# Twelve rows of the first block loaded through GpSimd's queue in transfers of 5, 120 and 3 partitions

## Chip, cores and metric

One core of one Trainium2 chip. The metric is the device time of one execution in microseconds (us), median of several executions. Times inside a run are us from the start of the profiled span, which is 1.2 to 1.7 us shorter than the device time.

## The reference

```python
W_adapted = W + scale * (lora_A @ lora_B)            # 256 x 256, rank 16
W_norm = np.sqrt(np.sum(W_adapted ** 2, axis=0, keepdims=True) + 1e-8)
W_final = W_adapted / W_norm * m
y = x.reshape(-1, 256) @ W_final                     # x: 16 x 2048 x 256 float32
```

The weights are small. The work is to read 33.5 MB of x, multiply it by a 256 x 256 matrix, and write 33.5 MB of y.

## The kernel before

x is cut into 8 blocks of 128 partitions x 32 rows x 1 KB (4 MB; the last is loaded and stored in two halves). There are five block buffers, and the result overwrites the block's buffer. SyncE (queue q1 in the profile) issues the loads, ACT (q10) the stores. GpSimd casts to bfloat16, TensorE transposes and multiplies, DVE and ACT move the results back.

```python
def load_x(n):
    nc.sync.dma_start(
        out=in_sbuf(*parts[n]), in_=in_dram(x_flat, *parts[n])
    ).then_inc(sem(f"load{n}"), 16)
...
for n in range(len(parts)):
    b = parts[n][0] // CH
    if b >= XBUFS and parts[n][0] % CH == 0:
        nc.sync.wait_ge(sem(f"store{b - XBUFS}"), 16)   # buffer free again
    load_x(n)
...
for p in range(NPR):                                    # GpSimd, four casts a block
    b, c = divmod(p, PRB)
    if p == 0 or part_of[2 * p - 1] != part_of[2 * p]:
        nc.gpsimd.wait_ge(sem(f"load{part_of[2 * p]}"), 16)
    if p >= NXB:
        nc.gpsimd.wait_ge(sem("turned"), p - NXB + 1)
    nc.gpsimd.tensor_copy(out=xb_bufs[p % NXB][:],
        in_=x_bufs[b % XBUFS][:, 2 * c * J : 2 * (c + 1) * J, :],
    ).then_inc(sem("rounded"), 1)
```

So loads 0 to 4 are issued at once, load 5 only when store 0 has landed, load 6 after store 1, and loads 7 and 8 after store 2.

## Time and profile before

| | before |
|---|---|
| device time, median of 3 runs | 164.33 us (163.7 to 165.0) |
| span of the profiled run | 163.2 us |
| mean DMA rate over the span | 413 GB/s |
| first cast / first store issued / last store issued | 13.83 / 34.52 / 148.20 us |

A line of the order of time gives start, duration, engine, line of the program, operation, and in brackets the engine's idle time before it with what ended it.

The stage of the early loads, in the table of stages whose columns the prediction explains:

```profile
12.00:32.00 20.00, 12.35 (x86) 10.38 (x87) 10.80 (x9) 5.60 (x6) 11.39 (x6) 1.00 0.99 426
```

Here only loads run, at 426 GB/s.

### The profile page before, as it was taken

Reading aid. Unit: us, or ns where it says so; the run is one execution under the profiler, and the core shown is the slowest. Engines: PE = TensorE matmul, PEld = TensorE weight load, DVE = VectorE, ACT = ScalarE, POOL = GpSimd, SP = SyncE. Lnnn points to the kernel's source line nnn. Section 1 sums busy time; section 2 is a strip of 40 time slices with the busy share of each in tenths; the row PEclk is TensorE's granted clock in tenths of the full one; section 3 lists DMA queues with packets and bytes.
Section 4 is the critical chain, followed back from the end, with each engine's and each line's share of the span. In section 5 each row is a group of like instructions: output and inputs, shape, how many; then the busy total and the mean of one; then the engine's idle time right before and its main releaser. Section 6 shows DMA issues by size and latency. Waiting matters only on the chain. (4 is left out here: it accounts for less than half of the span.)

```text
span 163.2 us, 1988 instructions
## 1 busy us (share of the span) xinstructions
PE 105.3 (65%) x786; PEld 85.2 (52%) x786; DVE 47.2 (29%) x44; ACT 63.8 (39%) x67; POOL 62.5 (38%) x39
## 2 busy tenths in 40 slices
PE   1270599789789897898981998619988820892000
PEld 0130577677577775776760867418676610771000
DVE  0429452350532514405230325005051400330000
ACT  3010027548366384473754053900738440062000
POOL 1006381753935738268004940069209003900000
PEclk9999999999999999999998589985899996599755
DMA  5998998998999999999999999999999999998991
GB/s 201 402 498 386 426 474 385 482 418 265 466 426 426 442 410 466 426 394 482 418 426 442 420 426 458 402 458 410 446 414 454 414 446 422 450 442 377 442 430 60
DMA packets 2915, 67.41 MB, mean 413 GB/s; under 512 B 465, under 2 KB 482, under 8 KB 610
## 3 DMA queue, kind: packets, MB, share of 16 engines
q1 hardware_dynamic: 1440, 33.82, 49.0%
q10 hardware_dynamic: 1474, 33.59, 47.8%
q14 instruction: 1, 0.01, 0.0%
HBM read 33.85 MB, written 33.55 MB: 413 GB/s over the span
## 5 line engine op out<-in xcount | busy, mean ns | idle before, releaser
L219 ACT COPY x_sb<-y_ps 128x1024 f32<-128x1024 f32 x64 | 61.9, 1014 | 75.8 <-PE y_ps L281 75.8
L165 POOL CAST xb<-x_sb 128x2048 bf16<-128x2048 f32 x32 | 60.0, 1902 | 79.3 <-DMA x_sb<-in_x_dram 56.0
L281 PE MATMUL y_ps<-w_final,xt 128*128 128x256 bf16 x512 | 64.6, 280 | 12.8 <-PEq L256 12.8
L202 DVE COPY xt<-xt_ps 128x1024 f32<-128x1024 f32 x32 | 38.2, 1221 | 88.1 <-PE xt_ps L267 88.0
L281 PEld LDWEIGHTS y_ps<-w_final,xt 128*128 128x128 bf16 x512 | 48.4, 100 | 28.2 <-issue 19.8
L267 PE MATMUL xt_ps<-identity,xb 128*128 128x128 f32 x264 | 39.1, 309 | 23.1 <-PEq L256 23.1
L267 PEld LDWEIGHTS xt_ps<-identity,xb 128*128 128x128 f32 x264 | 34.9, 161 | 25.8 <-issue 25.6
L198 DVE TENSOR_TENSOR w_final<-wam,rnorm 128x256 bf16<-128x256 f32 x2 | 4.0, 2028 | 0.0
L244 PE MATMUL y_ps<-sq,ones 128*128 128x256 f32 x4 | 2.1, 674 | 1.6 <-DVE sq L187 1.6
L233 PE MATMUL y_ps<-identity,a_nat 128*16 128x128 f32 x2 | 0.6, 397 | 3.6 <-DMA a_nat<-in_lora_A_dram 3.6
L212 ACT ACTIVATE norm<-y_ps,eps_col 128x256 f32<-128x256 f32 x1 | 0.5, 473 | 6.1 <-PE y_ps L244 6.1
L244 PEld LDWEIGHTS y_ps<-sq,ones 128*128 128x128 f32 x4 | 1.2, 323 | 2.3 <-DVE sq L187 2.1
L210 ACT ACT_TABLE_LOAD x1 | 1.3, 1283 | 2.4 <-issue 2.4
L233 PEld LDWEIGHTS y_ps<-identity,a_nat 128*16 128x16 f32 x2 | 0.1, 90 | 3.6 <-issue 3.6
L171 POOL MEMSET xb<- 128x2048 bf16 x1 | 1.8, 1805 | 0.3 <-PE xt_ps L267 0.3
L195 DVE RECIPROCAL rnorm<-norm 128x256 f32<-128x256 f32 x1 | 1.7, 1745 | 0.0
L237 PE MATMUL y_ps<-b_bf,aT 16*128 16x256 bf16 x2 | 0.6, 404 | 1.5 <-DVE aT L180 1.5
L189 DVE COPY m_all<-y_ps 128x256 f32<-128x256 f32 x1 | 0.4, 425 | 3.3 <-PE y_ps L249 3.3
L178 DVE CAST b_bf<-b_nat 16x256 bf16<-16x256 f32 x1 | 0.3, 281 | 3.8 <-DMA b_nat<-in_lora_B_dram 3.8
L249 PE MATMUL y_ps<-m_row,ones 1*128 1x256 f32 x2 | 1.2, 710 | 0.0
L237 PEld LDWEIGHTS y_ps<-b_bf,aT 16*128 16x128 bf16 x2 | 0.1, 106 | 1.9 <-DVE aT L180 1.9
L183 DVE SCALAR_TENSOR_TENSOR wa<-y_ps,w_nat 128x512 f32<-128x512 f32 x1 | 0.7, 692 | 0.8 <-PE y_ps L237 0.8
(13 smaller groups left out, 3.7 us busy)
## 6 DMA issues: line engine op xcount, KB each, us to landing
x_sb<-in_x_dram SPq DMA_DIRECT2D x7, 4096.0 KB, 27.1
out_dram<-x_sb ACTq DMA_DIRECT2D x7, 4096.0 KB, 37.2
x_sb<-in_x_dram SPq DMA_DIRECT2D x2, 2048.0 KB, 29.6
out_dram<-x_sb ACTq DMA_DIRECT2D x2, 2048.0 KB, 20.2
w_nat<-in_W_dram SPq DMA_DIRECT2D x1, 256.0 KB, 2.9
a_nat<-in_lora_A_dram ACTq DMA_DIRECT2D x1, 16.0 KB, 2.6
b_nat<-in_lora_B_dram ACTq DMA_DIRECT2D x1, 16.0 KB, 3.6
m_row<-in_m_dram ACTq DMA_DIRECT2D x1, 1.0 KB
```

The costliest lines, as they stand in the source:

```text
L165: nc.gpsimd.tensor_copy(out=xb_bufs[p % NXB][:], in_=x_bufs[b % XBUFS][:, 2 * c * J : 2 * (c + 1) * J, :],).then_inc(sem("rounded"), 1)
L171: nc.gpsimd.memset(xb_bufs[NPR % NXB][:], 0.0).then_inc(sem("rounded"), 1)
L183: nc.vector.scalar_tensor_tensor(out=wa[:], in0=ab_ps, scalar=float(scale), in1=w_nat[:], op0=ALU.mult, op1=ALU.add).then_inc(dv, 1)
L195: nc.vector.reciprocal(out=rnorm[:], in_=norm[:]).then_inc(dv, 1)
L198: i = nc.vector.tensor_mul(out=w_final[:, t], in0=wam[:, t], in1=rnorm[:])
L202: nc.vector.tensor_copy(out=xt_bufs[p % NXT][:].rearrange("p r t -> p (r t)").bitcast(FP32), in_=xt_ps[p % 2][:],).then_inc(sem("copied"), 1)
L210: nc.scalar.activation(out=warm[:], in_=eps_col[:], func=AF.Sqrt)
L219: nc.scalar.copy(out=x_bufs[b % XBUFS][:, c * J : (c + 1) * J, :], in_=y_ps[g % 2][:]).then_inc(sem("room"), 1)
L244: i = nc.tensor.matmul(n2_ps, ones[:], sq[:, t, :], start=(t == 0), stop=(t == KC - 1))
L249: nc.tensor.matmul(mb_ps, ones[0:1, :], m_row[:], start=True, stop=True).then_inc(pe, 1)
L267: i = nc.tensor.transpose(xt_ps[p % 2][:, j * P : (j + 1) * P], xb_bufs[p % NXB][:, j, :].bitcast(FP32), identity[:],)
L281: i = nc.tensor.matmul(y_ps[h][:, j, :], xt_bufs[p % NXT][:, r : r + P, t], w_final[:, t, :], start=(t == 0 and (j % (J // 2)) == 0), stop ...
```

## The change

One of the 16 DMA engines finishes the kernel later than the others. The intent is to give it less: 12 of 32 rows of block 0 are taken from the ordinary load, which is shared evenly, and loaded by GpSimd in three transfers arranged so that DMA engine 4 gets almost none of them.

```diff
+    EARLY = 12
+    SPARE = 4
+    SHARES = [(0, SPARE + 1), (SPARE + 1, 120), (SPARE + 121, 7 - SPARE)]
@@ load_x
+        s = EARLY if n == 0 else 0
         nc.sync.dma_start(
-            out=in_sbuf(*parts[n]), in_=in_dram(x_flat, *parts[n])
+            out=in_sbuf(*parts[n])[:, s:, :], in_=in_dram(x_flat, *parts[n])[:, s:, :]
         ).then_inc(sem(f"load{n}"), 16)
@@ GpSimd, after the identity and ahead of the casts
+    for k, (p0, cnt) in enumerate(SHARES):
+        nc.gpsimd.dma_start(
+            out=in_sbuf(*parts[0])[p0 : p0 + cnt, 0:EARLY, :],
+            in_=in_dram(x_flat, *parts[0])[p0 : p0 + cnt, 0:EARLY, :],
+            max_dma_last_dim=4096,
+        ).then_inc(sem(f"early{k}"), 16)
+    for k in range(len(SHARES)):
+        nc.gpsimd.wait_ge(sem(f"early{k}"), 16)
```

The cap of 4096 cuts each partition's 12 KB into three pieces.

## The prediction

> **What bounds the kernel now.** I read the page's slices first, then the table of stages, then the packets of two short windows, then the order of time on GpSimd and ACT.
>
> The slices (busy tenths of the mean DMA engine, and GB/s, in 40 equal parts of the span):
>
> ```profile
> DMA  5998998998999999999999999999999999998991
> GB/s 201 402 498 386 426 474 385 482 418 265 466 426 426 442 410 466 426 394 482 418 426 442 420 426 458 402 458 410 446 414 454 414 446 422 450 442 377 442 430 60
> ...
> q1 hardware_dynamic: 1440, 33.82, 49.0%
> q10 hardware_dynamic: 1474, 33.59, 47.8%
> ```
>
> See that the DMA engines are full from the second slice to the last but one, while no compute engine is over 65%: loads (q1) and stores (q10) take 96.8% of sixteen engines' span. So the time is bytes per DMA engine plus a start and a tail. Stages (us; busy time of PE, PEld, DVE, ACT, POOL with counts; granted clock; DMA share; GB/s):
>
> ```profile
> 114.00:135.00 21.00, 15.65 (x125) 12.23 (x123) 5.35 (x5) 11.76 (x12) 4.98 (x3) 0.96 1.02 439
> ...
> 148.50:159.40 10.90, 0.00 (x0) 0.00 (x0) 0.00 (x0) 0.00 (x0) 0.00 (x0) 0.71 0.99 424
> 159.40:160.50 1.10, 0.00 (x0) 0.00 (x0) 0.00 (x0) 0.00 (x0) 0.00 (x0) 0.50 0.25 104
> 160.60:162.70 2.10, 0.00 (x0) 0.00 (x0) 0.00 (x0) 0.00 (x0) 0.00 (x0) 0.50 0.05 23
> ```
>
> All compute is over by 148.5; then stores drain at full rate to 159.4, and from 160.6 to 162.7 the share is 0.05, about 1/16. One DMA engine works alone. Its packets:
>
> ```profile
> DMA packets 4, 0.05 MB, mean 23 GB/s; under 512 B 1, under 2 KB 1, under 8 KB 1
> ...
> q10 hardware_dynamic: 4, 0.05, 5.5%
> ```
>
> Three packets of 16 KB and one semaphore write. In the packet records (start and duration, without engine numbers) sixteen last-store semaphore writes end at 159.57 to 160.42 us, but the last at 162.78: a straggler 2.36 us behind the next. Following its packets back by end-meets-start, it never idles. It does its equal share more slowly: 32 KB packets that last 1.213 us elsewhere last 1.22 (loads) and 1.23 to 1.27 (stores) on it from 78 us on. The summed excess over 1.213 and 0.611 us is about 1.4 us after 78 us and 1.0 us around 48 us, when the stores come in (others pay much of the latter too). The lag shows growing in the store semaphores: last against last but one is 0.29 us at the first store (60.17) and 1.93 us at the seventh (142.94). That straggler is the thing the change aims at.
>
> How two queues share an engine matters below. From 106.9 to 121.9 us, 16 KB load packets meet 32 KB store packets:
>
> ```profile
> q10 hardware_dynamic: 147, 4.29, 66.4%
> q1 hardware_dynamic: 146, 2.11, 32.9%
> ```
>
> As many packets of each, twice the bytes of one: an engine alternates packet by packet, whatever their sizes. The 1 KB load of m shows it at the start: its last three packets on q10 lie 1.25 us apart, one 32 KB packet of q1 between each.
>
> When block 0 is needed (start, duration):
>
> ```profile
> 13.83 3.92 POOL L165 CAST xb<-x_sb 128x2048 bf16<-128x2048 f32 x2 [12.15 <-DMA x_sb<-in_x_dram]
> ```
>
> The first cast waits for load 0, landed at 13.42; the first store is issued at 34.52, 20.7 us after that cast starts.
>
> **What the Trainium skill says.** "DMA: Bandwidth & Descriptors", section "Why a DMA increments its semaphore by 16 and not by 1": a DMA uses the largest number of engines up to 16 that divides its slowest dimension; from GpSimd a smaller set starts at a round-robin cursor, first share on its lowest-numbered engine; but some direct copies get all 16 engines with partitions/16 rounded up on each. The kernel before has no GpSimd transfer, so its trace can't confirm either. Same page, "Queues, rings and completion order": engines round-robin between queues at packet granularity, a packet being some 9 to 17 descriptors. The trace agrees on the round-robin (147 against 146), with single rows as packets on these queues. Same page, "SWDGE vs HWDGE vs iDMA": a GpSimd packet is preferably at most 4096 B, at most 64 descriptors. That sits badly with the 9 to 17 when a descriptor is 4096 B, and it decides the rival below. No run here shows it.
>
> **The change part by part.** It removes 12 of 32 rows (12 KB of each partition's 32 KB) from load 0 and adds three GpSimd transfers of the same 1.5 MB, each row group cut into three pieces of 4 KB (the built kernel holds them as 5x3x1024, 120x3x1024, 3x3x1024). Total bytes stay; only their spread over engines changes.
>
> Spread, with the divisor rule and a cursor from 0: 5 partitions go to engines 0 to 4, one each; 120 to fifteen engines 5 to 15 and 0 to 3, eight each; 3 to engines 4, 5, 6. So engine 4 carries 2 partitions instead of 8, engines 0 to 3, 5 and 6 carry 9, the rest 8.
>
> - Byte rate: 16 KB per 0.607 us spacing, 32 KB per 1.210 us, so 0.0368 us per 1,000 B (difference over 16,384 B) and about 5 ns per packet.
> - Engine 4: 6 x 12,288 B less = 73,728 B = 2.71 us earlier. If it is the straggler, 162.78 becomes about 160.1.
> - Engines with 9: 12,288 B more = 0.45 us. The others' last is 160.42, so 160.4 to 160.9.
> - Pieces: 24 more packets per engine x 5 ns = 0.12 us, three more semaphore writes at 9 ns = 0.03 us.
> - New end of the stores: 160.6 to 161.0, against 162.78. Gain 1.8 to 2.2 us; I take 1.9.
> - GpSimd: three issues and waits before the first cast, some us in a stretch where it sits idle 12.15 us; off the path if the data lands in time.
>
> How much delay of block 0 is free? Loads 0 to 4 keep the engines busy alone until 3.5 + 5 x 9.75 = 52.2 us (loads land 9.7 us apart before stores begin). The first cast may slip to about 26 us before stores come too late to fill the engines. So the main path gains 1.9 us: 164.33 - 1.9 = 162.4 us.
>
> **The rivals.**
> 1. *The early part lands too late.* If every 4 KB piece takes one turn, an engine with 27 pieces and three semaphore writes needs 30 turns. From about 4 us: 8 turns beside the 20 KB rests of load 0, each 0.757 + 0.155 = 0.91, make 7.3 us; the other 22 fall beside load 1 and 2's 32 KB packets at 1.37 us, some 29 us. It would land near 40 us, not 13.4. The first cast slips 26 us, the first store to 60; engines idle from 52 to about 62, and some 2 us more before load 5, which waits for store 0. That is 12 us lost less 2 gained: about 174 us. For it: the 147 to 146 count, and 4096 B as preferred packet size. Against: the skill's typical packet of 9 to 17; if one turn takes three pieces (12 KB) there are about 12 turns and landing is near 15 us; two per turn lands near 25. Only strictly one piece per turn hurts. The amounts (73,728 B for a 2.36 us lag) look fitted to a measured straggler, which speaks for someone having watched it work.
> 2. *The wrong engine is relieved.* The trace before doesn't number engines. If 120 partitions go 8 each to engines 0 to 14, or the straggler isn't 4, it gains nothing or carries 9 to 10 partitions: 0 to 0.9 us later, 164.3 to 165.3 us.
> 3. *Another straggler takes over.* The next engine ends at 160.42, so at most 2.36 us can ever be won this way, 1.4%. A gain over 2% would need 3.3 us; nothing here offers it.
>
> **Range and chances.** Main path 0.63 (161.5 to 163.3 us), wrong or half relief 0.13 (163.3 to 165.5), late landing 0.21 (168 to 175), other 0.03. Point: 162.5 us. The distribution has two humps, so the range for 8 in 10 has to reach into the second: 161.2 to 170.5 us. Faster by over 2%: 0.03; within 2%: 0.75; slower by over 2%: 0.22.
>
> **What would show it.** In the profile after: a third queue with 1.57 MB in 384 packets of 4 KB; first cast still at 13 to 26 us (main) or near 40 us with two or three low DMA slices around 52 to 62 us (rival 1); the last slice without a stretch at a sixteenth of the DMA (main), or with that stretch kept at 2 us or more (rival 2); compute groups with unchanged durations. My number is wrong if the first cast starts after 30 us or if one engine still ends over 1.5 us after the others.

## More of the kernel before

ACT's first and last store issue, before:

```profile
34.52 0.37 ACTq L128 DMA_DIRECT2D out_dram<-x_sb  x1
...
148.20 0.34 ACTq L128 DMA_DIRECT2D out_dram<-x_sb  x1
```

## The result, and the profile after

The changed kernel takes 185.62 us (median of 4 runs, 184.62 to 186.57) against 164.01 us (4 runs). The ratio is 1.131, 95% interval 1.121 to 1.140: 13% slower. All ratios here are the mean time of one kernel's fast runs over that of the other's in the same rounds, so not quite the ratio of the medians quoted. The time lies far outside the predicted range.

The slices and queues after (the same lines that the prediction shows of before):

```profile
span 185.1 us, 1993 instructions
...
DMA  5998999999999005959999999999999999999994
GB/s 205 407 382 301 355 316 353 364 298 365 429 404 404 14 0 227 453 227 347 425 425 390 453 446 439 361 453 423 411 439 429 446 432 453 411 432 425 418 434 177
...
q0 software_dynamic: 528, 1.57, 2.6%
```

Three things are new: two empty slices from 60 to 69 us with half-empty ones after them, a rate of 298 to 365 GB/s from 14 to 46 us where the DMA engines count as busy, and the new queue q0. Its 528 packets are 384 pieces of 4 KB and 144 of 4 bytes. GpSimd and ACT in order of time, after:

```profile
2.02 2.11 POOL L167 DMA_DIRECT2D x_sb<-in_x_dram  x3 [0.34 <-issue]
53.44 3.72 POOL L180 CAST xb<-x_sb 128x2048 bf16<-128x2048 f32 x2 [49.32 <-DMA x_sb<-in_x_dram]
```

```profile
71.12 0.37 ACTq L135 DMA_DIRECT2D out_dram<-x_sb  x1
...
170.25 0.34 ACTq L135 DMA_DIRECT2D out_dram<-x_sb  x1
```

GpSimd is done issuing at 4.1 us and then waits 49.32 us for the early rows. (The three transfers land one after the other, at 11.3, 49.5 and 53.2 us; in the packet records the last semaphore write of the third ends at 52.8.) The first cast slips from 13.83 to 53.44 us, the first store from 34.52 to 71.12. Stages after:

```profile
24.00:50.00 26.00, 0.00 (x0) 0.00 (x0) 0.00 (x0) 0.00 (x0) 0.00 (x0) 1.00 1.01 353
50.00:60.00 10.00, 4.53 (x24) 4.06 (x25) 1.94 (x2) 0.00 (x0) 6.24 (x4) 1.00 0.98 417
61.00:71.50 10.50, 9.18 (x81) 7.90 (x80) 2.98 (x3) 6.96 (x8) 4.55 (x4) 1.00 0.00 0
81.70:83.40 1.70, 1.70 (x18) 1.46 (x16) 0.00 (x0) 1.40 (x3) 0.00 (x0) 1.00 0.01 0
...
182.70:184.20 1.50, 0.00 (x0) 0.00 (x0) 0.00 (x0) 0.00 (x0) 0.00 (x0) 0.50 0.08 33
```

From 24 to 50 us no engine computes at all. Loads 0 to 4 are over by 61.8 us; then the DMA engines have nothing to do until the first store, and once more until load 5, which waits for store 0. In the packet records no engine moves anything for 10.2 us and then for 1.5 us. In the last line one DMA engine again works alone: the last semaphore write ends at 184.55 us, the one before it at 183.05. The packets from 12 to 48 us:

```profile
q1 hardware_dynamic: 365, 10.91, 88.5%
q0 software_dynamic: 362, 1.34, 11.1%
```

As many packets of q0 as of q1: each 4 KB piece waits for a 32 KB packet of loads that nobody needs yet. This is the prediction's first rival, and more severe than it said.

**Theory A**, then: the early part takes one turn of the round-robin per piece and so lands near 53 us; the first cast and the first store slip with it; the time is the late first store, nothing else. **Theory B**: the GpSimd transfers slow the DMA engines (353 against 426 GB/s), and this is part of the loss of its own. A third question is whether the relief of engine 4 would have been right at all.

### The profile page after: what moved, and what is told of

The parts are those of the page before. It is cut to its first block, busy times and chain, and to the rows that moved or that the text cites. A ratio compares the mean times of both kernels' runs of the same rounds, so it can differ in the third digit from the quotient of the medians.

```text
span 185.1 us, 1993 instructions
## 1 busy us (share of the span) xinstructions
PE 98.9 (53%) x786; PEld 81.0 (44%) x786; DVE 43.6 (24%) x44; ACT 63.6 (34%) x67; POOL 64.4 (35%) x42
## 5 line engine op out<-in xcount | busy, mean ns | idle before, releaser
L296 PE MATMUL y_ps<-w_final,xt 128*128 128x256 bf16 x512 | 62.0, 273 | 14.8 <-PEq L271 14.8
L217 DVE COPY xt<-xt_ps 128x1024 f32<-128x1024 f32 x32 | 37.9, 1220 | 114.0 <-PE xt_ps L282 114.0
L282 PE MATMUL xt_ps<-identity,xb 128*128 128x128 f32 x264 | 35.3, 291 | 50.0 <-PEq L271 50.0
L296 PEld LDWEIGHTS y_ps<-w_final,xt 128*128 128x128 bf16 x512 | 47.1, 98 | 29.0 <-issue 21.8
L282 PEld LDWEIGHTS xt_ps<-identity,xb 128*128 128x128 f32 x264 | 32.1, 151 | 51.7 <-issue 51.5
L167 POOL DMA_DIRECT2D x_sb<-in_x_dram x3 | 2.1, 704 | 0.3 <-issue 0.3
L264 PEld LDWEIGHTS y_ps<-m_row,ones 1*128 1x128 f32 x2 | 0.5, 308 | 0.7 <-issue 0.7
## 6 DMA issues: line engine op xcount, KB each, us to landing
x_sb<-in_x_dram SPq DMA_DIRECT2D x1, 2560.0 KB, 11.3
```

The source lines that it names most:

```text
L167: nc.gpsimd.dma_start(out=in_sbuf(*parts[0])[p0 : p0 + cnt, 0:EARLY, :], in_=in_dram(x_flat, *parts[0])[p0 : p0 + cnt, 0:EARLY, :], max_dm ...
L217: nc.vector.tensor_copy(out=xt_bufs[p % NXT][:].rearrange("p r t -> p (r t)").bitcast(FP32), in_=xt_ps[p % 2][:],).then_inc(sem("copied"), 1)
L264: nc.tensor.matmul(mb_ps, ones[0:1, :], m_row[:], start=True, stop=True).then_inc(pe, 1)
L282: i = nc.tensor.transpose(xt_ps[p % 2][:, j * P : (j + 1) * P], xb_bufs[p % NXB][:, j, :].bitcast(FP32), identity[:],)
L296: i = nc.tensor.matmul(y_ps[h][:, j, :], xt_bufs[p % NXT][:, r : r + P, t], w_final[:, t, :], start=(t == 0 and (j % (J // 2)) == 0), stop ...
```

## The experiments

### late_block0: the late first cast without any of the change

```diff
 # the kernel before
+    nc.gpsimd.wait_ge(sem("load4"), 16)
     for p in range(NPR):
```

> The kernel before with one line more: GpSimd waits for load 4 as well before its first cast; no GpSimd transfer at all. Theory A (only the late first cast costs, the slower DMA engines beside it cost nothing more): first cast near 52.5 us, first store near 70, and from there the pace of the changed kernel (8 more stores at 13.2 us a block, then a drain of 14 us), so about 183 to 186 us. Theory B (the GpSimd pieces themselves slow the DMA engines, and that is part of the 22 us): clearly less, about 175 us.

Measured: 185.78 us, ratio 1.135 (1.132 to 1.139). Its stages:

```profile
12.00:48.00 36.00, 0.00 (x0) 0.00 (x0) 2.79 (x5) 0.00 (x0) 0.00 (x0) 1.00 0.99 427
52.20:70.50 18.30, 14.49 (x107) 12.31 (x108) 4.84 (x5) 7.60 (x8) 11.19 (x7) 1.00 0.00 0
```

The first cast starts at 52.64 and the first store is issued at 70.71 us. The DMA engines keep their full 427 GB/s, yet the time is that of the changed kernel: they only idle longer (19.4 us instead of 10.2, by the packet records). So lateness alone accounts for the whole loss, and the slower DMA rate of the changed kernel lies in a stretch that would have been idle. Theory B falls for this kernel.

### late_load1 and late_load2: how much lateness is free

The same line with `load1` (lands near 23 us) or `load2` (near 33 us).

> The kernel before, with GpSimd waiting for load 1 too before its first cast (lands near 23 us). If lateness of block 0 is free up to about 26 to 31 us: first cast near 23.3 us, first store near 42 us, total within 0.5% of the kernel before. If each microsecond of lateness cost one from the start: about 173 us.

> The same with load 2 (lands near 33 us). In all late kernels so far the end came 113.5 to 114 us after the first store was issued. First cast near 33 us, first store near 51 us, so a span near 164.7 us, 1 to 1.5 us above the kernel before: just past the end of the free stretch. If there is no such stretch: 9 us above late_load1.

Measured: 163.90 us, ratio 1.000 (0.997 to 1.003), and 166.76 us, ratio 1.019 (1.015 to 1.022). First stores:

```profile
41.94 0.37 ACTq L128 DMA_DIRECT2D out_dram<-x_sb  x1
```

```profile
51.66 0.37 ACTq L128 DMA_DIRECT2D out_dram<-x_sb  x1
```

Ten microseconds of lateness cost nothing, the next nine cost 2.9 us. (I had expected up to 1.5 us; the before runs of this chip were nearer to a span of 162 us than 163.) The reason is plain when all late kernels, those below included, are put together:

| kernel | first cast | first store | span | span less first store |
|---|---|---|---|---|
| before | 13.83 | 34.52 | 163.2 | 128.7 |
| late_load1 | 23.72 | 41.94 | 162.4 | 120.5 |
| late_load2 | 33.09 | 51.66 | 165.2 | 113.5 |
| act_queue | 35.69 | 53.50 | 167.1 | 113.6 |
| sw_128 | 35.70 | 54.02 | 167.5 | 113.5 |
| sw_2x64 | 43.41 | 60.88 | 174.6 | 113.7 |
| sw_6k | 43.18 | 61.63 | 175.2 | 113.6 |
| late_block0 | 52.64 | 70.71 | 184.3 | 113.6 |
| act_split | 53.40 | 70.98 | 184.4 | 113.4 |
| changed kernel | 53.44 | 71.12 | 185.1 | 114.0 |

From the first store on, the late kernels keep one schedule. In the changed kernel stores 0 to 6 go out 13.2 us apart, the pace of the computing (71.12 to 150.46 us; GpSimd waits for TensorE). Then GpSimd waits 3.64 us for load 7 and 10.96 us for load 8, the last half block; both had been held until store 2 had landed. So the last store goes out at 170.25, 99 us after the first, and its drain takes some 14.5. All of this moves with the first store. With a first store ahead of about 49 us (163 - 113.6), the DMA engines' bytes set the end instead.

### act_queue and sw_128: is it GpSimd's queue?

Both load the 12 rows as one transfer of 128 partitions in 4 KB pieces: act_queue on ACT's queue behind the load of m, sw_128 on GpSimd's.

```diff
-    SHARES = [(0, SPARE + 1), (SPARE + 1, 120), (SPARE + 121, 7 - SPARE)]
+    SHARES = [(0, 128)]
 # act_queue: nc.gpsimd.dma_start -> nc.scalar.dma_start, after the load of m_row
```

> The changed kernel with its early part as one 128-partition transfer in the same 4 KB pieces, but on ACT's queue. Theory A (one piece per turn of the round-robin, whatever queue it is on): 24 pieces and one semaphore write are 25 turns, landing between 33 us (32 KB packets stay at 1.21 us, a turn of 1.37 us) and 40 us (they are stretched to 1.5 us as beside GpSimd's pieces), total 165 to 172 us. Theory C (only GpSimd's queue is starved): landing before 20 us, total near 164 us.

> The changed kernel with its early part as one GpSimd transfer of 128 partitions in 4 KB pieces: 24 pieces and one semaphore write per engine, no 4-byte padding[...]. Theory A with a turn of 1.74 us: about 25 turns from 6.5 us, landing near 45 us, total near 176 us. If the stretched 32 KB packets came from engines writing unusual partitions: a turn of 1.37 us, landing near 38 us, total near 170 us. Theory C' (the three-way split itself is the trouble): landing before 20 us.

Measured: 168.93 us, ratio 1.032 (1.028 to 1.037), and 168.91 us, ratio 1.032 (1.029 to 1.035). Packets from 12 to 32 us, act_queue and then sw_128:

```profile
q1 hardware_dynamic: 242, 7.41, 85.8%
q10 hardware_dynamic: 241, 0.99, 12.0%
```

```profile
q1 hardware_dynamic: 241, 7.37, 85.5%
q0 software_dynamic: 240, 0.98, 11.9%
```

One piece per 32 KB packet on either queue, so landing is near 35 us on both (first cast at 35.7). (Of the totals named for sw_128, 176 and 170 us, the lower came nearer.) Theory C, that only GpSimd's queue is starved, falls; so does C', that only the three-way split starves the pieces, since a single transfer is late too. In the records the 32 KB packets last 1.215 us and the pieces 0.159 us in the mean, a turn of 1.37 us as the prediction worked out, and the DMA moves 420 and 418 GB/s. In the changed kernel the same packets last 1.53 and 0.195 us. The last piece ends 17 us earlier here (34.0 against 51.0 us); the split has to explain that, and longer packets are only a part of it. In the changed kernel the 120 partitions' pieces start near 9.5 instead of 6.4 us, after the turns of the small transfer ahead of them, and the small transfer behind them lands 3.7 us after them (53.2 against 49.5). That is some 7 of the 17 us; the rest is left to longer turns.

### sw_6k: fewer, larger pieces

```diff
-            max_dma_last_dim=4096,
+            max_dma_last_dim=6144,
```

> The changed kernel with pieces of 6 KB instead of 4 KB, otherwise the same three transfers. Theory A (a turn per piece): 2 pieces per partition instead of 3, some 23 turns instead of 33, landing near 40 us instead of 53, total near 172 us. Theory D (bytes, not pieces, set the landing): landing stays near 53 us, total near 185 us.

Measured: 176.24 us, ratio 1.077 (1.073 to 1.081). First cast:

```profile
43.18 3.72 POOL L180 CAST xb<-x_sb 128x2048 bf16<-128x2048 f32 x2 [39.18 <-DMA x_sb<-in_x_dram]
```

The same bytes in two thirds of the pieces land 10 us earlier. Turns count, not bytes alone; theory D falls. The gain is less than in proportion because a turn is longer: 32 KB packets take 1.62 and pieces 0.31 us from 13 to 39 us.

This kernel also shows who takes part. It has 112 packets of 4 bytes on q0, the changed kernel 144, sw_2x64 (below) 32 and sw_128 16. Sixteen per transfer are the semaphore writes. The rest fits exactly if every DMA engine that a transfer leaves out gets one 4-byte packet for each piece of a participant: with 5, 15 and 3 engines taking part, 11 x 3 + 1 x 24 + 13 x 3 = 96 = 144 - 48, and 11 x 2 + 16 + 13 x 2 = 64 = 112 - 48. So the intended split did happen. In the changed kernel's records some twenty of these come singly between 11.8 and 43.4 us, 1.5 to 1.8 us apart: the engine left out takes its turns as well, with nothing in them. So every engine there has 3 + 24 + 3 pieces or empty packets and 3 semaphore writes, 33 turns, against 25 in sw_128.

### sw_2x64 and act_split: what stretches the packets?

```diff
 # sw_2x64, on GpSimd's queue
+    SHARES = [(0, 64), (64, 64)]
 # act_split, on ACT's queue
+    SHARES = [(0, 5), (5, 120), (125, 3)]
```

> The changed kernel with its early part as two GpSimd transfers of 64 partitions each in 4 KB pieces: all 16 engines, no padding, 26 turns[...]. Theory P (unusual partitions stretch the packets): 32 KB packets at 1.4 to 1.6 us and pieces near 0.19 us while both run, landing near 44 us, total 175 to 178 us. Theory Q (the fifteen-engine split and its 4-byte padding stretch them): packets at 1.21 us, pieces 0.16 us, landing near 36 us, total near 169 us.

> The early part in the changed kernel's transfers of 5, 120 and 3 partitions and 4 KB pieces, but all on ACT's queue. If the stretched packets come from engines writing partitions that are not theirs: 32 KB packets near 1.5 us while the pieces run, DMA near 350 GB/s, landing 45 to 50 us, total 177 to 182 us. If they come from GpSimd's own queue when split: packets at 1.21 us and landing near 36 to 38 us, total 169 to 171 us.

Measured: 176.34 us, ratio 1.077 (1.072 to 1.083), and 185.32 us, ratio 1.131 (1.123 to 1.139). Packets of sw_2x64 from 12 to 40 us, and the stage of act_split:

```profile
DMA packets 607, 10.06 MB, mean 359 GB/s; under 512 B 48, under 2 KB 48, under 8 KB 336
## 3 DMA queue, kind: packets, MB, share of 16 engines
q1 hardware_dynamic: 303, 8.88, 89.0%
q0 software_dynamic: 304, 1.18, 11.3%
```

```profile
12.00:36.00 24.00, 0.00 (x0) 0.00 (x0) 3.38 (x6) 0.00 (x0) 0.00 (x0) 1.00 0.98 350
```

act_split has no GpSimd transfer, and runs as slowly as the changed kernel: the three-way split on ACT's queue costs 16.4 us over the single transfer on the same queue (185.32 against 168.93). I had expected 177 to 182 us. Its 32 KB packets take 1.46 us from 12 to 32 us, those of act_queue 1.215. So the split stretches the packets, not the queue (how much of the 16.4 us is stretch and how much additional turns, I did not separate). sw_2x64 has neither a fifteen-engine split nor packets for engines left out, and its 32 KB packets still take 1.47 us in the mean. This supports theory P, that engines write other partitions than in a transfer of 128, and speaks against Q. The Trainium skill, "DMA: Bandwidth & Descriptors", section "The descriptor swizzle", says that in a 128-partition transfer each engine writes the partitions of one SBUF port of its own, and gives this division for that shape; "SBUF — State Buffer", section "Door 1: The DMA port swizzle", gives the ports. Two engines writing through one port would be a reason. But if that were all, the packets of the engines whose own partitions lie above 63 would keep 1.215 us while sw_2x64's first transfer, to partitions 0 to 63, runs; of the 112 load packets that start from 10 to 23 us none is under 1.4 us. So why a split stretches every engine's packets stays open; the records name neither engines nor ports. That the division of partitions sets the rate is measured.

### gate_load1: the early part without the 32 KB packets beside it

```diff
         if b >= XBUFS and parts[n][0] % CH == 0:
             nc.sync.wait_ge(sem(f"store{b - XBUFS}"), 16)
+        if n == 1:
+            for k in range(len(SHARES)):
+                nc.sync.wait_ge(sem(f"early{k}"), 16)
         load_x(n)
```

> The changed kernel, with the issuing of load 1 held until all three early transfers have landed, so that their 4 KB pieces only meet the 20 KB rests of load 0. Theory A (lateness through turns beside 32 KB packets): the bulk of the pieces starts near 9.5 us when the rests are nearly done, 24 pieces and padding take 4 to 6 us, landing near 16 us, first store near 37 us; the DMA engines lose some 3 us between, the relief gives back up to 2: total 164 to 167 us, 19 us or more below the changed kernel. If the lateness came from GpSimd's descriptor making instead, landing would stay beyond 40 us and the total near 180 us or more.

Measured: 171.23 us, ratio 1.046 (1.042 to 1.050). Stage and first cast:

```profile
9.00:20.00 11.00, 1.48 (x3) 0.50 (x2) 3.61 (x6) 0.47 (x1) 0.94 (x1) 1.00 0.74 172
```

```profile
19.06 3.72 POOL L183 CAST xb<-x_sb 128x2048 bf16<-128x2048 f32 x2 [14.93 <-DMA x_sb<-in_x_dram]
```

The first cast comes at 19 us and 14 us of the loss are gone, with the same transfers and the same descriptor making. That confirms the turns. But the total missed my 164 to 167 us: the pieces alone last 0.306 us in the mean, nearly twice the 0.159 of sw_128, and 11 us at 172 instead of some 426 GB/s lose about 6.6 us of DMA time (11 x (1 - 172/426)). (No run holds load 1 behind a single transfer of 128 partitions, so how much of this the split costs and how much the pieces being alone, is not shown.) Now the first store is early (37.69 us), DMA bytes bound the kernel, and the slow rate does cost.

### blk3_s4 and blk3_s12: the relief without the lateness

The same three transfers in 6 KB pieces, taken out of block 3, which is cast much later; blk3_s12 first moves the cursor by a tiny transfer of 8 partitions, so that engine 12 is left out.

```diff
+    HELP = 3                                  # block 3 in place of block 0
-        s = EARLY if n == 0 else 0
+        s = EARLY if n == HELP else 0
-            max_dma_last_dim=4096,
+            max_dma_last_dim=6144,
+        if p == HELP * PRB:                   # the wait moves to block 3's first cast
+            for k in range(len(SHARES)):
+                nc.gpsimd.wait_ge(sem(f"early{k}"), 16)
 # parts[HELP] for parts[0] in the transfers; blk3_s12 also SPARE = 12 and the tiny transfer
```

> The same three GpSimd transfers in 6 KB pieces, but taken out of block 3, which is cast from 54 us on, not out of block 0. Theory A: no late first cast (near 14 us), landing near 43 us, no wait for the early part. If the stretched packets cost DMA time that nothing hides here: some 9 us of engine time lost in the load stage less up to 2.4 us of relief, total 168 to 172 us. If only the late cast mattered: 162 to 163 us. If DMA engine 4 is the straggler, the last stores end with no engine more than 0.8 us behind the next.

> As blk3_s4, but a tiny transfer of 8 partitions first moves the cursor, so that engine 12 is left out instead of engine 4. If engine 4 is the straggler: an engine ends 2 us or more behind the next at the end and the total is 1 to 2.5 us above blk3_s4. If another engine is, or none in particular: no difference to blk3_s4 within 0.8 us.

Measured: 172.02 us (172.0 to 173.99), ratio 1.055 (1.048 to 1.062), and 173.41 us (172.37 to 174.84), ratio 1.062 (1.055 to 1.069). First cast and a stage of blk3_s4:

```profile
17.76 3.72 POOL L182 CAST xb<-x_sb 128x2048 bf16<-128x2048 f32 x2 [13.76 <-DMA x_sb<-in_x_dram]
```

```profile
12.00:42.00 30.00, 19.79 (x148) 16.41 (x149) 9.09 (x9) 10.78 (x12) 14.88 (x8) 1.00 1.00 345
```

No lateness here; the first store goes out at 36.04 us and the early part has landed by 46.4, long before block 3's first cast at 65.2. Still 8 us are lost: 30 us at 345 instead of 426 GB/s are 5.7 us of DMA time, and the late loads delay the last store to 163.4 us (148.2 before); from 160 to 164 us the DMA engines are almost idle (share 0.09). blk3_s12 has 312 GB/s in the same stage. Where DMA bytes bound the kernel, theory B holds after all.

The total does not tell the two kernels apart (the intervals overlap), and the sign that I had set for blk3_s12, an engine 2 us or more behind at the end, did not come: the last engine is 0.31 us behind the next, 0.49 in blk3_s4. In both kernels most engines had run dry before the last store was issued, so the ending says nothing of a straggler. I then looked at the load semaphores. Lead of the first DMA engine (taken to be the one left out, as the records have no numbers) over the second, us, worked out from the semaphore writes in the packet records:

| landing of load | 2 | 3 | 4 | 5 | 6 | 7 |
|---|---|---|---|---|---|---|
| blk3_s4, engine 4 left out | 3.15 | 2.82 | 2.40 | 2.12 | 1.83 | 1.54 |
| blk3_s12, engine 12 left out | 5.07 | 5.07 | 5.07 | 5.07 | 5.07 | 5.07 |

An engine that leads keeps its lead if it is as fast as the next. Engine 12 keeps it; engine 4 gives up 1.6 us between load 2 and load 7. The other fifteen engines agree: in blk3_s4 they keep their distances within 0.02 us from load 3 to load 5, and one slips once, at load 6, by about 0.6; in blk3_s12 one of them falls back steadily, 0.86, 1.14, 1.39 and 1.63 us behind the first of the fifteen at loads 4 to 7. So one engine is slow, it is the one that the change relieves, and the intent had its target right, on the chip of this run at least. The number 4 rests on the prediction's rule and a cursor from 0; no record shows it. At load 8, the last half block, the leads are 1.13 and 2.65 us: there the second shrinks too, and I can't say why, nor why the two differ in size from the start.

No run points to a version that beats the kernel before: every form of the split that was tried costs more DMA time than the 2.4 us that there are to win, and the even transfers relieve nobody.

## Why the prediction was wrong, point by point

- **What bounds the kernel before** (bytes per DMA engine, one straggler 2.36 us behind): nothing measured contradicts it. late_load1 adds that ten microseconds of lateness leave the time alone.
- **The spread over engines** (5, 15 and 3 engines from a cursor): right. The 4-byte packets fit it, and in the changed kernel one engine lands load 4 at 58.03 us, 2.24 us ahead of the next.
- **The gain of 1.9 us**: never collected. The lead is lost when all engines idle from about 60 to 72 us, and 1.5 us of straggling grow anew by the end (184.55 against 183.05).
- **The failed step: "off the path if the data lands in time".** I gave late landing 0.21, though the count of 147 to 146 packets in the kernel before had shown the alternation packet by packet, and the pieces were cut to 4 KB. I weighed against it the skill's typical packet of 9 to 17 descriptors and the guess that the amounts were fitted to a measured straggler. Runs showed one piece per turn: 362 against 365 in the changed kernel, 240 against 241 in sw_128.
- **The size of that rival**: about 174 us was said, 185.62 measured. The term at fault is the landing, "near 40 us", which was 52.8. First, the bulk of the pieces starts near 9.5 us, not 4, when the 20 KB packets are nearly over. Second, a turn is 1.53 + 0.195 = 1.73 us, not 1.37, because of the split; 24 turns from 9.5 us give 51, and the second transfer landed at 49.5 (a few of its pieces met a 4-byte semaphore write in place of a 32 KB packet). Third, the last transfer takes its turns after that; with the empty packets an engine has 33 turns, not 30. Two sums were off as well: 22 turns at 1.37 us are 30 us, not 29, and three pieces a turn would by the same terms have landed near 19 us, not 15, still within the free delay. The sign named in advance, a first cast after 30 us, came true at 53.44. The chain behind the landing held: a first store at the predicted 60 us plus 114 gives 174, at the measured 71.1 plus 114 it gives 185.
- **The free delay** of the first cast, "about 26 us": right to within the steps tried, free at 23.7 and 2.9 us lost at 33.1; by the table it ends near 31 us.
- **"Only strictly one piece per turn hurts"**: true, but larger pieces still hurt: 6 KB ones lost 7.7%.
- **Rivals 2 and 3** (wrong engine, another straggler): not what happened. blk3_s4 and blk3_s12 speak for engine 4.

## What to carry to other kernels

In these runs a transfer on a second queue was served packet by packet against the first, so its landing time was about its number of turns times the packet time of whatever else was queued, not its bytes over the rate; put nothing urgent in small pieces beside a deep queue of large ones. Judge a delay by the first point where it empties a queue: here, by the table, a first cast up to about 31 us was free, and beyond that each microsecond cost one. And before splitting a transfer unevenly over DMA engines, measure the rate of the split itself: one engine's 2.4 us were the prize, and the split cost some 6 us of DMA time in the two places where it was not hidden (5.7 in blk3_s4; 6.6 in gate_load1, not all of it surely the split's).

## What the Trainium skill lacked or had wrong

- "DMA: Bandwidth & Descriptors", "Queues, rings and completion order" has packets of some 9 to 17 descriptors as the unit of the round-robin. Here every piece took its own turn, on GpSimd's queue as on ACT's: 240 against 241 and 241 against 242 packets in 20 us.
- No page has the 4-byte packets of data, beside the semaphore writes, that engines left out by a GpSimd transfer get: 96 of the 528 packets of q0 in the changed kernel. Each takes a turn.
- Same page, "Rules for kernel authors" says of two transfers to disjoint partition halves that they serialize and are not worth it, not that they slow other transfers. Here two of 64 partitions ran at 359 GB/s where one of 128 ran at 418, 176.34 against 168.91 us; the 5, 120 and 3 split in 4 KB pieces ran at 350 to 353 GB/s. No page says that such a transfer lengthens the packets of another queue, here those of 32 KB from 1.215 to 1.47 us.
- Same page, "Latency and other measured facts" names DMA engines 7 and 15 as usually slower, for GpSimd transfers. Here it was the engine that the change leaves out, number 4 if the cursor starts at 0, with a loss of 1.6 us of lead over five loads, nearly all in a stretch where GpSimd's transfers were over.
